# Pauses in the decode batches and the gates, sums of squares on a third engine, and another last norm in a one-layer hybrid decoder step

## The chip, the cores and the metric

The kernel runs on one core of a Trainium2 chip. The core has a matmul engine (PE, with its weight loads shown apart as PEld), a vector engine (DVE), a scalar engine (ACT), GpSimd (POOL), a queue engine (SP) and 16 DMA engines. The metric is the device time of one execution in microseconds (us), the median of several runs.

## The reference

One inference step of one decoder layer: a half-weight SwiGLU FFN, a combined projection into mLSTM heads (4 of 128) and sliding-window attention (8 heads of 64, window 128), an output projection, and a second half-weight FFN, each with an RMSNorm before and after it. 1024 prompt rows and 8 decode sequences of 4 rows go through the same weights; D_MODEL is 1024, D_FF 2816. All is float32.

```python
def half_ffn(x, j, gpre, gpost):
    y = swiglu(rmsnorm(x, g[gpre]), ffn_w_gate[l, j], ffn_w_up[l, j], ffn_w_down[l, j])
    return x + 0.5 * rmsnorm(y, g[gpost])

x = half_ffn(x, 0, 0, 1)
h = rmsnorm(x, g[2])
(qm, km, vm, om, ip, fp), (qa, ka, va) = split_proj(h, w_in[l], b_gate[l])
u_m, new_m = mlstm_heads(qm, km, vm, om, ip, fp, mstate, mlstm_norm_gain[l], h.dtype)
u_a, new_kv = swa_prompt(...)            # swa_sample(...) for the decode rows
u = jnp.concatenate([u_m, u_a], axis=-1)
x = x + rmsnorm(u @ w_out[l], g[3])
x = half_ffn(x, 1, 4, 5)
```

The mLSTM of the decode rows starts from a given state C (128x128) and n for each of 8 sequences and 4 heads, reads it (q @ C) and writes the new one:

```python
num = a[..., None] * jnp.einsum('bhtk,bhkv->bhtv', q, C) + jnp.einsum('bhts,bhsv->bhtv', S, v)
C_new = decay[..., None, None] * C + jnp.einsum('bhs,bhsk,bhsv->bhkv', wk, k, v)
```

## The kernel before

The 1056 rows stand in columns, in four quarters q0 to q3 of 264 (256 of the prompt and 8 of decode), with the 1024 features over partitions in pairs of blocks (kp 0 to 3, tiles of 128x528). A float32 product is made of three passes of a faster float format, from a high and a low part of each operand (xh, xl for rows, wh, wl for weights), so most matmuls come in threes, all through one helper line, L163. Transposes have L160, the split into parts L206 (ACT, the high part) and L207 (DVE, the low part).

The phases are FFN1 (tiles gu, pd, and pl where a product waits for late rows), the middle or mix (pz, pv and po are columns of the input projection, for z, v and the output gate; sws, swp and swo are the attention; E, S, intra, inter and U the mLSTM of the prompt; pw is the output projection, of uh and ul, the parts of the head outputs), FFN2, and the last norm.

What stands where on an engine is set by a hand-made clock (class `Order`). Each side job is a generator that is given a start and yields a number of us of PE time. Every matmul that the main loop issues moves the clock on by its price, and side jobs that are due are stepped in between, so a `yield 2.6` means that some 2.6 us of matmuls of the main loop come before the job goes on. The engines then run their instructions in order, and wait for each other by semaphores. `issue_after` is an order alone: an instruction isn't placed ahead of another on its engine.

The jobs that the change touches:

- `post()` ends a phase for a quarter q: residual add (y, L606 and L607), squares on ACT, their sum over kp in `acc` (sq, L615), the halves (L250), the sums over partitions on PE with the rows turned (cs) and a reduce on DVE (L260), a reciprocal square root by two Newton steps in `rstd()` (L280 to L289, tiny operations; "newton" below), and its broadcast over partitions on PE (rb). The next phase's quarter waits for that row. `late` is true for all quarters of phase 2 (end of the mix) and for q2 and q3 of phase 1 (end of FFN1).
- `gates()` makes the decays of the mLSTM for a group of four chunks; each chunk has two transposes (gT) and a copy into `K.cols`.
- `mlstm_sample()` runs the decode rows of the mLSTM over pairs of sequences: read (sinter, from the states Cb), then for each pair of heads the update (sU on PE, L1885 on DVE). After the four pairs comes a head (sintra, snum, a norm, shT), and its turned result is copied by ACT (L1915) into the columns of z that later become uh and ul.
- `Last.finish()` is the tail after the last matmul of FFN2.

```python
            for b, ps, Cb in zip(bs, pu, C):
                for x in range(2):
                    h = 2 * hp + x
                    nc.vector.scalar_tensor_tensor(Cb[:, h], Cb[:, h], K.dec[:, 1, h, b:b + 1],
                                                   ps[:, x * 129:(x + 1) * 129], op0=ALU.mult, op1=ALU.add)
            yield BW
```

Of the kernel before, what the change touches and what calls it, by code (L numbers as in the profile page):

```python
# [14 lines left out]
ALU = mybir.AluOpType  # L15
# [27 lines left out]

BW = 2.4

# [13 lines left out]
def setup(ctx, tc, A, O):  # L59
# [17 lines left out]

    K.h, K.room = {}, 1000
    K.ident = K.cp.tile([P, P], F32, tag="ident", name="ident")
    make_identity(nc, K.ident)  # L80
# [99 lines left out]
def pair(t):  # L180
    return t.rearrange("p (a t) -> p a t", a=2)
# [18 lines left out]
def small(K, name, w):  # L200
    return K.kp.tile([P, 8], F32, tag="c", name=nm(K, name), bufs=16)[:, 0:w]
# [71 lines left out]

def rstd(K, ss, scale=1.0 / D, eps=EPS, root=False):


    nc = K.nc
    w = ss.shape[-1]
    v, r, t, u = [small(K, x, w) for x in ("v", "r", "rt", "ru")]
    nc.vector.tensor_scalar(v, ss, scale, eps, op0=ALU.mult, op1=ALU.add)  # L280
    nc.vector.tensor_scalar(r.bitcast(I32), v.bitcast(I32), -0.5, float(0x5F3759DF), op0=ALU.mult, op1=ALU.add)

    nc.vector.tensor_tensor(t, r, v, op=ALU.mult)
    nc.vector.tensor_tensor(t, t, r, op=ALU.mult)
    nc.vector.scalar_tensor_tensor(u, t, -10.0 / 3.0, t, op0=ALU.add, op1=ALU.mult)
    nc.vector.scalar_tensor_tensor(r, u, 5.0, r, op0=ALU.add, op1=ALU.mult)
    nc.vector.scalar_tensor_tensor(t, r, -0.5 * 0.375 ** 3, v, op0=ALU.mult, op1=ALU.mult)
    nc.vector.tensor_tensor(t, t, r, op=ALU.mult)
    nc.vector.scalar_tensor_tensor(r, t, 1.5 * 0.375, r, op0=ALU.add, op1=ALU.mult)  # L289
    if not root:  # L290
        return r
    nc.vector.tensor_tensor(u, v, r, op=ALU.mult)
    return r, u
# [288 lines left out]
def post(K, phase, q, y, acc, half, nxt, gpre=None):  # L582
# [22 lines left out]
    for kp in range(4):  # L605
        nc.vector.tensor_tensor(pair(y[kp]), pair(y[kp]), cr.unsqueeze(1).to_broadcast([P, 2, QW]), op=ALU.mult)  # L606
        nc.vector.tensor_tensor(y[kp], y[kp], x[kp], op=ALU.add)  # L607
        if nxt:
            stash(K, q, kp, y[kp])
            sq = tmp(K, "sq", 2 * QW)  # L610
            nc.scalar.square(sq, y[kp])
            if acc is None:
                acc = sq
            else:
                nc.vector.tensor_tensor(acc, acc, sq, op=ALU.add)  # L615
        if nxt == "mix":
# [15 lines left out]
    yield PW[3]  # L632
    r = rstd(K, col_stats(K, sq, phase))
    yield PW[4][late]
    if nxt == "mix":
# [36 lines left out]
class Last:  # L672
# [30 lines left out]
    def block(self, mo, ps):  # L703
# [14 lines left out]
        if mo == 6:  # L718
            K.od.spawn(self.stats(0), 2.0)
        if mo == 3:  # L720
# [3 lines left out]

    def stats(self, i):

        ss = col_stats(self.K, self.acc[i], 3)
        if i:
            self.K.nc.vector.tensor_tensor(ss, ss, self.ss, op=ALU.add)
        self.ss = ss  # L730
        yield 0
# [21 lines left out]

    def finish(self):
        K, q = self.K, self.q
        for _ in self.stats(1):
            pass
        K.od.drain()

        c = rstd(K, self.ss, 4.0 / D, 4.0 * EPS)  # L760
        for j in range(3):
            for x in range(2):
                o = tmp(K, "yo", 512)
                if j < 2:
                    K.nc.vector.scalar_tensor_tensor(o, self.y[j][x], c[:, j:j + 1], self.x[j][x], op0=ALU.mult,
                                                     op1=ALU.add)
                    dst = K.O["y_prompt"][0, (2 * q + j) * P:(2 * q + j + 1) * P]
                else:
                    r = slice(96, P)
                    K.nc.scalar.activation(o[r], self.y[j][x][r], AF.Copy, scale=c[r, j:j + 1])  # L770
                    K.nc.vector.tensor_tensor(o[r], o[r], self.x[j][x][r], op=ALU.add)
                    o = o[120:128]
                    dst = K.O["y_sample"].rearrange("b t d -> (b t) d")[8 * q:8 * q + 8]
                K.nc.sync.dma_start(dst[:, x * 512:(x + 1) * 512], o)

# [618 lines left out]
def gates(K, n):  # L1394
# [28 lines left out]
    for c, o in chunks:  # L1423
        ps = bank(K, "gT", "b")
        pe(K, ps[:, 0:100], G[0:100, o:o + P], K.ident[0:100, 0:100], tr=True)
        pe(K, ps[:, P:P + 4], I[:, o:o + P], K.ident[0:4, 0:4], tr=True)
        nc.vector.tensor_copy(K.cols[:, c], ps[:, 0:160].rearrange("p (y s) -> p y s", s=32)[:, :, 0:4])
    K.od.done.add(("gates", n))

# [393 lines left out]
def mlstm_sample(K):  # L1823
# [41 lines left out]
    for b0 in range(0, 8, 2):  # L1865
# [3 lines left out]
        for b, Cb in zip(bs, C):  # L1869
            for h in range(HM):  # L1870
                q = qm[h // 2][:, (h % 2) * 256 + b * 32:(h % 2) * 256 + b * 32 + 32]
                pe(K, pi[32 * h:32 * h + 32, 0:129], q, Cb[:, h], start=(b == 0), stop=(b == 7),
                   tile_position=(0, 32 * h))
        for hp in range(2):
            pu = [bank(K, "sU", "ba"[hp]) for b in bs]
# [6 lines left out]
            for b, ps, Cb in zip(bs, pu, C):  # L1882
                for x in range(2):
                    h = 2 * hp + x
                    nc.vector.scalar_tensor_tensor(Cb[:, h], Cb[:, h], K.dec[:, 1, h, b:b + 1],  # L1885
                                                   ps[:, x * 129:(x + 1) * 129], op0=ALU.mult, op1=ALU.add)
            yield BW
        for b, Cb in zip(bs, C):
# [323 lines left out]
```

## Time and profile before

| | us |
|---|---|
| median of 3 runs | 1978.07 (1975.69 to 1980.95) |
| the profiled execution | 1979.65, its span 1977.9 |
| PE busy | 1953.1 (99% of the span) |
| DVE busy | 1251.7 (63%) |
| ACT busy | 903.9 (46%) |
| POOL busy | 42.9 (2%) |

The mean granted clock of PE is 0.993 of full speed. In the profile an engine's row says how long it was occupied; matmuls overlap, so the durations of single ones (0.28 us) are longer than the distance from one to the next. A view by windows gives busy time, the clock and the DMA share for each stretch of time. In the order of an engine below, a name's number tells tiles of the same kind apart, and x2 means two alike in a row.

### The profile page before, as it was taken

To read this page: it belongs to the slowest core of one execution; us is meant where nothing else is said; L and a number is where in the kernel's file an instruction comes from. 1 tells how busy PE (TensorE), PEld (TensorE's weight loads), DVE (VectorE), ACT (ScalarE), POOL (GpSimd) and SP (SyncE) were. 2 spreads that over 40 slices of the span, in tenths; PEclk is the share of its full clock that TensorE was granted. 3 is DMA by queue.
4 is the path that set the end of the run, shared out by engine and by line. 5 is a ranking of instruction groups with operands and counts; after the bars stand their busy time and mean duration, and the time that the engine had idled before them with its cause. 6 is when DMAs were issued, how large, how long until landed. Compare 5 with 4: busy or idle time off the path is not lost.

```text
span 1977.9 us, 40244 instructions
## 1 busy us (share of the span) xinstructions
PE 1953.1 (99%) x15897; PEld 1912.3 (97%) x15897; DVE 1251.7 (63%) x2986; ACT 903.9 (46%) x2167; POOL 42.9 (2%) x193
## 2 busy tenths in 40 slices
PE   8999999999999999999999999999999999999998
PEld 8999999999999999987999999999999999999997
DVE  8755555557568437467565768985555555856774
ACT  7533333336456332356244665353333334645563
POOL 1000000000000002000101000000000000000000
PEclk9999999999999999999999899999999999999999
DMA  7123222226357352201224234322222222746693
GB/s 251 55 76 116 92 76 84 74 92 207 97 161 240 109 146 84 63 1 38 79 65 131 64 108 136 121 84 91 76 89 86 97 76 82 218 122 199 206 265 121
DMA packets 283583, 226.42 MB, mean 114 GB/s; under 512 B 22441, under 2 KB 256033, under 8 KB 283393
## 3 DMA queue, kind: packets, MB, share of 16 engines
q1 hardware_dynamic: 283392, 223.84, 36.6%
q8 instruction: 124, 2.03, 0.4%
q14 instruction: 67, 0.54, 0.1%
HBM read 175.70 MB, written 47.89 MB: 113 GB/s over the span
## 4 chain that ended last, share of the span: by engine, by line
PE 91%; DVE 4%; ACT 2%; DMA 1%; issue 1%; SPq 0%; DVEq 0%; ACTq 0%
PE gu L163 41%; PE pd L163 25%; PE pz L163 6%; PE pw L163 4%; PE pl L163 3%; PE pv L163 3%; PE po L163 3%; DMA hq<-h 1%; PE sws L163 1%; PE swo L163 1%; PE yT L160 1%; ACT sws L1524 0%; PE swp L160 0%; PE U L163 0%; DVE y L607 0%
## 5 line engine op out<-in xcount | busy, mean ns | idle before, releaser
L163 PE MATMUL gu<-Xh,wh 128*128 128x264 f32 x2240 | 636.0, 284 | 1.5 <-ACT sc L1023 1.5
L163 PE MATMUL gu<-Xl,wh 128*128 128x264 f32 x2240 | 636.9, 284 | 0.0
L163 PE MATMUL gu<-Xh,wl 128*128 128x264 f32 x2240 | 636.2, 284 | 0.0
L163 PE MATMUL pd<-hq,wh 128*128 128x264 f32 x2752 | 509.3, 286 | 1.2 <-ACT sc L1127 1.2
L163 PEld LDWEIGHTS pd<-hq,wh 128*128 128x128 f32 x2752 | 426.7, 188 | 1.8 <-ACT sc L1127 1.6
L163 PEld LDWEIGHTS gu<-Xh,wh 128*128 128x128 f32 x2240 | 421.7, 188 | 2.0 <-ACT sc L1023 1.9
L163 PEld LDWEIGHTS gu<-Xh,wl 128*128 128x128 f32 x2240 | 421.7, 188 | 0.0
L163 PEld LDWEIGHTS gu<-Xl,wh 128*128 128x128 f32 x2240 | 421.0, 188 | 0.0
L207 DVE TENSOR_TENSOR wl<-raw,wh 128x512 fp32r<-128x512 f32 (+1 forms) x442 | 289.7, 667 | 163.1 <-ACT wh L206 144.4
L163 PE MATMUL pd<-hq,wl 128*128 128x264 f32 x1376 | 391.4, 284 | 0.0
L206 ACT CAST wh<-raw 128x512 fp32r<-128x512 f32 (+1 forms) x442 | 259.9, 601 | 248.8 <-PE pd L163 103.9
L163 PEld LDWEIGHTS pd<-hq,wl 128*128 128x128 f32 x1376 | 258.7, 188 | 0.0
L1023 ACT COPY sc<-gu 128x264 f32<-128x264 f32 x240 | 91.0, 380 | 354.1 <-PE gu L163 334.0
L207 DVE TENSOR_TENSOR wl<-ws,wh 128x512 fp32r<-128x512 f32 x192 | 130.5, 689 | 91.3 <-ACT wh L206 87.8
L1034 DVE TENSOR_TENSOR h<-gu,sc 128x264 f32<-128x264 f32 x120 | 51.8, 432 | 137.1 <-PE gu L163 86.0
L206 ACT CAST wh<-ws 128x512 fp32r<-128x512 f32 x192 | 115.0, 622 | 7.0 <-DVE ws L800 5.8
L1040 DVE TENSOR_TENSOR sc<-gu,sc 128x264 f32<-128x264 f32 x120 | 51.7, 431 | 95.9 <-PE gu L163 47.9
L163 PE MATMUL pz<-xh,wh 128*128 128x264 f32 x352 | 102.9, 292 | 0.6 <-DVE z L2085 0.6
L163 PE MATMUL pz<-xl,wh 128*128 128x264 f32 x352 | 101.3, 288 | 0.0
L163 PE MATMUL pz<-xh,wl 128*128 128x264 f32 x352 | 101.3, 288 | 0.0
L1035 ACT ACTIVATE h<-h 128x264 f32<-128x264 f32 x120 | 51.0, 425 | 107.7 <-DVE h L1034 107.7
L206 ACT CAST hq<-hq 128x264 fp32r<-128x264 f32 x192 | 70.9, 412 | 23.0 <-DMA hq<-h 19.4
(420 smaller groups left out, 3051.8 us busy)
## 6 DMA issues: line engine op xcount, KB each, us to landing
raw<-ffn_w_down SPq DMA_DIRECT2D x64, 512.0 KB
h<-h SPq DMA_DIRECT2D x84, 264.0 KB
raw<-ffn_w_gate SPq DMA_DIRECT2D x42, 512.0 KB
raw<-ffn_w_up SPq DMA_DIRECT2D x42, 512.0 KB
hq<-h SPq DMA_DIRECT2D x160, 132.0 KB
raw<-ffn_w_down SPq DMA_DIRECT2D x40, 384.0 KB
x<-xs SPq DMA_DIRECT2D x48, 264.0 KB
raw<-w_in SPq DMA_DIRECT2D x21, 512.0 KB
```

What stands on the lines that cost most here:

```text
L160: K.nc.tensor.transpose(out, lhsT, rhs)
L163: ins = K.nc.tensor.matmul(out, lhsT, rhs, start=start, stop=stop, **kw)
L206: K.nc.scalar.copy(hi, src)
L207: (eng or K.nc.vector).tensor_tensor(lo, src, hi.bitcast(F32), op=ALU.subtract)
L1023: nc.scalar.copy(sc[n][:, g], ps)
L1034: nc.vector.tensor_tensor(d, bk[tg, g], sc[n][:, g], op=ALU.add)
L1035: nc.scalar.activation(d, d, AF.Silu)
L1040: nc.vector.tensor_tensor(sc[n][:, g], src, sc[n][:, g], op=ALU.add)
```

## The change

Five edits. The decode batches pause also between read and update (2.6), and 1.9 instead of 2.4 after each half of the update. The gates pause 1.0 after each chunk. In `post()`, where rows are wanted soon (`late`), the adds of the squares of kp 1 and 2 go from DVE to POOL, and in q3 the multiply and the residual add of a kp stand behind the newton of q2, if that has been written by then. The last norm sums the squares over partitions by three matmuls against a column of ones and takes the earlier sum in as a ready-made column (`rest`), writes its first prompt chunk in two halves, and does the decode rows first, with POOL for the add and ACT's queue for the DMA.

```diff
...
 NP = [1.6, 3.0]
 GW = 10.0
-BW = 2.4
+BW = [2.6, 1.9]
 NPLAIN = 1
...
     K.X, K.b, K.S = [None] * NQ, [None] * NQ, [None] * NG
     K.h, K.room = {}, 1000
+    K.chain = None
     K.ident = K.cp.tile([P, P], F32, tag="ident", name="ident")
     make_identity(nc, K.ident)
     K.ones = K.cp.tile([P, 1], F32, tag="ones", name="ones")
...
     return ps[:, 0:QW]
-def rstd(K, ss, scale=1.0 / D, eps=EPS, root=False):
+def rstd(K, ss, scale=1.0 / D, eps=EPS, root=False, rest=None):
     nc = K.nc
     w = ss.shape[-1]
     v, r, t, u = [small(K, x, w) for x in ("v", "r", "rt", "ru")]
-    nc.vector.tensor_scalar(v, ss, scale, eps, op0=ALU.mult, op1=ALU.add)
+    if rest is None:
+        nc.vector.tensor_scalar(v, ss, scale, eps, op0=ALU.mult, op1=ALU.add)
+    else:
+        nc.vector.scalar_tensor_tensor(v, ss, scale, rest, op0=ALU.mult, op1=ALU.add)
     nc.vector.tensor_scalar(r.bitcast(I32), v.bitcast(I32), -0.5, float(0x5F3759DF), op0=ALU.mult, op1=ALU.add)
     nc.vector.tensor_tensor(t, r, v, op=ALU.mult)
...
     nc.vector.scalar_tensor_tensor(r, u, 5.0, r, op0=ALU.add, op1=ALU.mult)
     nc.vector.scalar_tensor_tensor(t, r, -0.5 * 0.375 ** 3, v, op0=ALU.mult, op1=ALU.mult)
     nc.vector.tensor_tensor(t, t, r, op=ALU.mult)
-    nc.vector.scalar_tensor_tensor(r, t, 1.5 * 0.375, r, op0=ALU.add, op1=ALU.mult)
+    K.newton = nc.vector.scalar_tensor_tensor(r, t, 1.5 * 0.375, r, op0=ALU.add, op1=ALU.mult).ins
     if not root:
         return r
     nc.vector.tensor_tensor(u, v, r, op=ALU.mult)
...
     acc = None
     g, i = q // 2, q % 2
     for kp in range(4):
-        nc.vector.tensor_tensor(pair(y[kp]), pair(y[kp]), cr.unsqueeze(1).to_broadcast([P, 2, QW]), op=ALU.mult)
-        nc.vector.tensor_tensor(y[kp], y[kp], x[kp], op=ALU.add)
+        with K.tc.issue_after(K.chain) if late and q == 3 and K.chain else nullcontext():
+            nc.vector.tensor_tensor(pair(y[kp]), pair(y[kp]), cr.unsqueeze(1).to_broadcast([P, 2, QW]), op=ALU.mult)
+            nc.vector.tensor_tensor(y[kp], y[kp], x[kp], op=ALU.add)
         if nxt:
             stash(K, q, kp, y[kp])
             sq = tmp(K, "sq", 2 * QW)
...
             if acc is None:
                 acc = sq
             else:
-                nc.vector.tensor_tensor(acc, acc, sq, op=ALU.add)
+                e = nc.gpsimd if kp < 3 and late else nc.vector
+                e.tensor_tensor(acc, acc, sq, op=ALU.add)
         if nxt == "mix":
             for k in (2 * kp, 2 * kp + 1):
                 s = slice((k % 2) * QW, (k % 2) * QW + QW)
...
     sq = halves(K, acc, phase)
     yield PW[3]
     r = rstd(K, col_stats(K, sq, phase))
+    K.chain = K.newton if late and q == 2 else None
     yield PW[4][late]
     if nxt == "mix":
         rc = K.kp.tile([P, 3], F32, tag=f"rc{q}", name=nm(K, "rc"), bufs=1)
...
             self.acc.append(sq)
         nc.scalar.activation(y, ps, AF.Copy, scale=gain)
         if mo == 6:
-            K.od.spawn(self.stats(0), 2.0)
+            K.od.spawn(self.stats(), 2.0)
         if mo == 3:
             K.od.spawn(self.first(self.t), 5.0)
         elif mo > 3:
             K.od.spawn(self.second(mo, y), 3.0)
-    def stats(self, i):
-        ss = col_stats(self.K, self.acc[i], 3)
-        if i:
-            self.K.nc.vector.tensor_tensor(ss, ss, self.ss, op=ALU.add)
-        self.ss = ss
+    def stats(self):
+        ss = col_stats(self.K, self.acc[0], 3)
+        self.rest = small(self.K, "ss", 3)
+        self.K.nc.vector.tensor_scalar(self.rest, ss, 4.0 / D, 4.0 * EPS, op0=ALU.mult, op1=ALU.add)
         yield 0
     def first(self, t):
...
         yield 0
     def finish(self):
         K, q = self.K, self.q
-        for _ in self.stats(1):
-            pass
+        nc = K.nc
+        ss = sbank(K, "cs")
+        for j, w in enumerate(WIN):
+            pe(K, ss[:, j:j + 1], self.acc[1][:, w:w + P], K.ones)
         K.od.drain()
-        c = rstd(K, self.ss, 4.0 / D, 4.0 * EPS)
-        for j in range(3):
+        c = rstd(K, ss[:, 0:3], 4.0 / D, rest=self.rest)
+        r = slice(96, P)
+        ys = K.O["y_sample"].rearrange("b t d -> (b t) d")[8 * q:8 * q + 8]
+        o = [tmp(K, "yo", 512) for _ in range(2)]
+        for x in range(2):
+            nc.scalar.activation(o[x][r], self.y[2][x][r], AF.Copy, scale=c[r, 2:3])
+        for x in range(2):
+            nc.gpsimd.tensor_tensor(o[x][r], o[x][r], self.x[2][x][r], op=ALU.add)
+            nc.scalar.dma_start(ys[:, x * 512:(x + 1) * 512], o[x][120:128])
+        for j in range(2):
+            dst = K.O["y_prompt"][0, (2 * q + j) * P:(2 * q + j + 1) * P]
             for x in range(2):
                 o = tmp(K, "yo", 512)
-                if j < 2:
-                    K.nc.vector.scalar_tensor_tensor(o, self.y[j][x], c[:, j:j + 1], self.x[j][x], op0=ALU.mult,
-                                                     op1=ALU.add)
-                    dst = K.O["y_prompt"][0, (2 * q + j) * P:(2 * q + j + 1) * P]
-                else:
-                    r = slice(96, P)
-                    K.nc.scalar.activation(o[r], self.y[j][x][r], AF.Copy, scale=c[r, j:j + 1])
-                    K.nc.vector.tensor_tensor(o[r], o[r], self.x[j][x][r], op=ALU.add)
-                    o = o[120:128]
-                    dst = K.O["y_sample"].rearrange("b t d -> (b t) d")[8 * q:8 * q + 8]
-                K.nc.sync.dma_start(dst[:, x * 512:(x + 1) * 512], o)
+                for a in ((0, 256), (256, 512)) if j + x == 0 else ((0, 512),):
+                    f = slice(*a)
+                    nc.vector.scalar_tensor_tensor(o[:, f], self.y[j][x][:, f], c[:, j:j + 1], self.x[j][x][:, f],
+                                                   op0=ALU.mult, op1=ALU.add)
+                    nc.sync.dma_start(dst[:, x * 512 + a[0]:x * 512 + a[1]], o[:, f])
...
         pe(K, ps[:, 0:100], G[0:100, o:o + P], K.ident[0:100, 0:100], tr=True)
         pe(K, ps[:, P:P + 4], I[:, o:o + P], K.ident[0:4, 0:4], tr=True)
         nc.vector.tensor_copy(K.cols[:, c], ps[:, 0:160].rearrange("p (y s) -> p y s", s=32)[:, :, 0:4])
+        yield 1.0
     K.od.done.add(("gates", n))
...
                 q = qm[h // 2][:, (h % 2) * 256 + b * 32:(h % 2) * 256 + b * 32 + 32]
                 pe(K, pi[32 * h:32 * h + 32, 0:129], q, Cb[:, h], start=(b == 0), stop=(b == 7),
                    tile_position=(0, 32 * h))
+        yield BW[0]
         for hp in range(2):
             pu = [bank(K, "sU", "ba"[hp]) for b in bs]
             for x in range(2):
...
                     h = 2 * hp + x
                     nc.vector.scalar_tensor_tensor(Cb[:, h], Cb[:, h], K.dec[:, 1, h, b:b + 1],
                                                    ps[:, x * 129:(x + 1) * 129], op0=ALU.mult, op1=ALU.add)
-            yield BW
+            yield BW[1]
         for b, Cb in zip(bs, C):
             nc.gpsimd.tensor_copy(nn[:, b], Cb[:, :, P])
             nc.sync.dma_start(O["s_C"][0, b].rearrange("h k v -> k h v"), Cb[:, :, 0:P])
```

PE in the middle of the decode batches, before. kw and vs make the update sU, Cb and qm the read sinter; po is the main loop's projection of the output gate.

```order
L163 MATMUL sinter_14003<-Cb_13917,qm_13995 32x129 x2
L163 MATMUL sinter_14003<-Cb_13917,qm_13999 32x129 x2
L163 MATMUL sU_14126<-vs,kw_13962 128x129 x2
L163 MATMUL sU_14127<-vs,kw_13962 128x129 x2
L163 MATMUL po_14104<-xh_1538_9805,wh_13753 128x264
L163 MATMUL sU_14136<-vs,kw_13962 128x129 x2
L163 MATMUL po_14104<-xl_1539_9806,wh_13753 128x264
L163 MATMUL po_14104<-xh_1538_9805,wl_13754 128x264
```

And the like place after:

```order
L164 MATMUL sU_14106<-vs,kw_13960 128x129
L164 MATMUL sU_14107<-vs,kw_13960 128x129
L164 MATMUL sU_14106<-vs,kw_13960 128x129
L164 MATMUL sU_14107<-vs,kw_13960 128x129
L164 MATMUL po_14072<-xh_1558_9876,wh_13757 128x264
L164 MATMUL po_14072<-xl_1559_9877,wh_13757 128x264
L164 MATMUL po_14072<-xh_1558_9876,wl_13758 128x264
L164 MATMUL po_14120<-xh_1530_9777,wh_13753 128x264
L164 MATMUL po_14120<-xl_1531_9778,wh_13753 128x264
L164 MATMUL po_14120<-xh_1530_9777,wl_13754 128x264
L164 MATMUL po_14120<-xh_1532_9781,wh_13753 128x264
L164 MATMUL po_14120<-xl_1533_9782,wh_13753 128x264
```

Before, sinter and sU follow each other with one or two po between them; after, a group of four sU is followed by a run of 12 po, of which the first eight are shown.

ACT behind shT, before, from the last copy out of it. num and hn belong to the prompt's mLSTM, og to the output gate, wh to a weight:

```order
L1915 COPY z_13851<-shT_14361 128x2x8
L206 CAST wh_14521<-raw_14517 128x512
L1760 ACTIVATE num_14407<-inter_14411,cols 128x129
L206 CAST uh_14403<-z_12798 128x528
L1760 ACTIVATE num_14407<-inter_14411,cols 128x129
L206 CAST wh_14525<-raw_14517 128x512
L206 CAST uh_14421<-z_12863 128x528
L206 CAST uh_14438<-z_12928 128x528
L1760 ACTIVATE num_14407<-inter_14431,cols 128x129 x2
L206 CAST uh_14454<-z_12993 128x528
```

After, from the last copy again:

```order
L1930 COPY z_13851<-shT_14449 128x2x8
L1774 ACTIVATE num_14495<-inter_14499,cols 128x129
L2076 ACT_TABLE_LOAD
L2076 ACTIVATE og_14287<-og_14287 128x528
L207 CAST uh_14491<-z_12780 128x528
L1774 ACTIVATE num_14495<-inter_14499,cols 128x129
L1696 ACTIVATE hn_14559,mss_14561<-num_14403 128x128
L207 CAST uh_14509<-z_12863 128x528
L1696 ACTIVATE hn_14559,mss_14561<-num_14403 128x128
L207 CAST wh_14715<-raw_14711 128x512
L207 CAST uh_14526<-z_12928 128x528
```

The casts uh that make the head outputs are now behind a table load and an og, and stand among the num and hn. On PE the shT stands as follows, after:

```order
L164 MATMUL pw_14598<-uh_13948,wh_14067 128x264
L164 MATMUL pw_14598<-ul_13949,wh_14067 128x264
L164 MATMUL pw_14598<-uh_13948,wl_14068 128x264
L164 MATMUL intra_14496<-v_10478,E_14347 128x129
L164 MATMUL intra_14496<-v_10482,E_14347 128x129
L164 MATMUL pw_14598<-uh_13967,wh_14067 128x264
L161 MATMUL shT_14449<-ident,snum_14376 128x128
L164 MATMUL pw_14598<-ul_13968,wh_14067 128x264
L164 MATMUL inter_14499<-C,z_13647 128x129
L164 MATMUL pw_14598<-uh_13967,wl_14068 128x264
L164 MATMUL pw_14598<-uh_13980,wh_14067 128x264
```

Before, some 90 rows of PE stood between shT and the first pw; now shT stands behind the first four pw, and pw of the decode heads' uh_14491 comes 25 rows after it.

DVE at the start of FFN2 (the sums of q2's squares, and the reduce and first step of q1's newton), before:

```order
L615 TENSOR_TENSOR sq_16323<-sq_16323,sq_16354 128x528
L992 TENSOR_TENSOR h_16149<-h_16149,pl_16253 128x264
L615 TENSOR_TENSOR sq_16323<-sq_16323,sq_16372 128x528
L260 TENSOR_REDUCE ss_16329<-cs_16325 128x3
L615 TENSOR_TENSOR sq_16323<-sq_16323,sq_16388 128x528
L280 TENSOR_SCALAR v_16331<-ss_16329 128x3
L992 TENSOR_TENSOR h_16195<-h_16195,pl_16300 128x264
L250 TENSOR_TENSOR sq_16323<-sq_16323 128x264
```

And after:

```order
L1005 TENSOR_TENSOR h_16149<-h_16149,pl_16253 128x264
L261 TENSOR_REDUCE ss_16329<-cs_16325 128x3
L622 TENSOR_TENSOR sq_16323<-sq_16323,sq_16388 128x528
L282 TENSOR_SCALAR v_16331<-ss_16329 128x3
L1005 TENSOR_TENSOR h_16195<-h_16195,pl_16300 128x264
L251 TENSOR_TENSOR sq_16323<-sq_16323 128x264
L285 TENSOR_SCALAR r_16332<-v_16331 128x3
L287 TENSOR_TENSOR rt_16333<-r_16332,v_16331 128x3
```

The two adds of kp 1 and 2 are gone from DVE (they are on POOL), and the third add, of kp 3, stands between q1's reduce and the first step of its newton.

## The prediction

> **What bounds the kernel now.** I read the busy times first, then the chain that ended last, then the waits of PE, and last the windows in which the granted clock falls.
>
> ```profile
> PE 1953.1 (99%) x15897; PEld 1912.3 (97%) x15897; DVE 1251.7 (63%) x2986; ACT 903.9 (46%) x2167; POOL 42.9 (2%) x193
> PE 91%; DVE 4%; ACT 2%; DMA 1%; issue 1%; SPq 0%; DVEq 0%; ACTq 0%
> ```
>
> PE is busy for 1953.1 of the 1977.9 us of the span and carries 91% of the chain. The change takes no matmul of weight off PE, so it can win in three places only: where PE waits, where PE runs at half clock, and in the tail after the last matmul. The waits of PE, all of the span:
>
> ```profile
> PE rb L160 <- DVE r L289: 3.2, 5, 1.5
> PE cs L160 <- DVE sq L250: 2.0, 1, 2.0
> PE pz L163 <- DVE z L2085: 0.6, 1, 0.6
> PE sU L163 <- DVE Cb L1885: 0.5, 1, 0.5
> ```
>
> The columns are total, times and longest. These are the waits on which the change acts, 6.3 us together: the stats of a norm (cs, rb), a projection (pz) and the decode states (sU). The half clock costs as much. Busy times by window; PEclk is the third number from the end:
>
> ```profile
> core 0: us, PE busy (x) PEld busy (x) DVE busy (x) ACT busy (x) POOL busy (x), PEclk, DMA share, GB/s
> 956.57:959.98 3.41, 3.41 (x23) 2.74 (x22) 0.89 (x5) 0.28 (x2) 0.00 (x0) 1.00 0.64 181
> 959.98:963.39 3.41, 3.41 (x18) 3.29 (x17) 2.37 (x20) 0.00 (x0) 0.19 (x1) 0.50 0.20 52
> 1086.27:1089.68 3.41, 3.41 (x35) 2.58 (x35) 2.39 (x10) 0.00 (x0) 0.38 (x2) 1.00 0.75 221
> 1089.68:1099.92 10.24, 10.24 (x63) 9.12 (x64) 3.43 (x12) 0.59 (x1) 0.76 (x4) 0.50 0.32 97
> 1260.36:1263.77 3.41, 0.84 (x7) 0.66 (x7) 3.39 (x9) 1.65 (x3) 0.00 (x0) 1.00 0.63 238
> 1263.77:1267.18 3.41, 3.41 (x18) 3.41 (x17) 3.41 (x8) 0.63 (x1) 0.00 (x0) 0.50 0.00 0
> ```
>
> Three stretches run at 0.50: 3.41 us at the gates, 10.24 us in the decode batches, 3.41 us at the start of FFN2. Half the time in each is lost: 1.7, 5.1 and 1.7 us. Before the third, PE was nearly idle (0.84 of 3.41). Before the other two it reads as busy, so I looked at what was in them, the full-width po matmuls alone:
>
> ```profile
> 1082.86:1086.27 3.41, 1.51 (x8) 1.10 (x8) 0.00 (x0) 1.00 0.82 239
> 1086.27:1089.68 3.41, 0.90 (x3) 0.48 (x3) 0.00 (x0) 1.00 0.75 221
> ```
>
> With 8 po matmuls in a window the next one kept the full clock; with 3 (and 32 narrow ones of the decode states) it lost it. My reading is that narrow matmuls count for little in whatever grants the clock. It rests on these two windows.
>
> **The change, part by part.** All against the profiled execution: 1979.65 us, span 1977.9; this is 1.6 above the median of the runs, 1978.07.
>
> *Decode batches.* The pauses put 9 to 12 po matmuls between the groups of sinter and sU, where there were 1 to 3. A full-width matmul comes every 0.12 us (1128.34 to 1128.46 below), so by the order every 3.41 us would hold about 12, more than the 8 that kept the clock. Taken: the 10.24 us stretch goes, −5.1 (ends: 0 if it stays, −5.1). The sU wait goes too, −0.5 (row above).
>
> *What the longer batches push back.* The decode head (shT) now stands inside the first pw matmuls. Before, it had 15 us of po matmuls behind it:
>
> ```profile
> 1113.50 0.33 PE L160 MATMUL shT<-ident,snum 128*128 128x128 f32 x1
> 1128.34 0.28 PE L163 MATMUL pw<-uh,wh 128*128 128x264 f32 x1
> 1128.46 0.28 PE L163 MATMUL pw<-ul,wh 128*128 128x264 f32 x1
> 1106.01 1.28 ACT L2061 ACT_TABLE_LOAD   x1
> 1107.31 0.64 ACT L2061 ACTIVATE og<-og 128x528 f32<-128x528 f32 x1
> 1113.92 0.71 ACT L1915 COPY z<-shT 128x16 f32<-128x16 f32 x8 [0.17 <-PE shT L160]
> 1116.70 0.62 ACT L206 CAST uh<-z 128x528 fp32r<-128x528 f32 x1
> 1117.38 0.37 ACT L1760 ACTIVATE num<-inter,cols 128x129 f32<-128x129 f32 x1
> 1121.61 0.31 ACT L1682 ACTIVATE hn<-num 128x128 f32<-128x128 f32 x1
> 1122.51 0.70 DVE L207 TENSOR_TENSOR ul<-z,uh 128x528 fp32r<-128x528 f32 x1
> ```
>
> Now ACT has, from shT: 0.42 to the first copy, copies 0.71, num 0.37, a table load 1.28 with og 0.64 (a like pair stood ahead of shT before, at 1106.01), and uh 0.62: first uh at +4.0. PE has 20 pw matmuls (2.4 us) and eight small ones (E counts four; some 0.1 each) until it needs it: 3.2. It stalls 0.8. For the other three heads ACT has three more casts, three hn (0.31, some 0.43 with the read of its sum), two num and one weight cast of 0.62: some 4.5, then the last ul 0.70: +9.2. PE's 32 rows to there hold 20 pw and 12 small ones, 3.9; it arrives at 7.1. Stall in all about 2.1. I take +2.0 (ends: 0, if ACT overlaps more; +8.0, if PE gets only the 3.2 done ahead of a chain of 11.2, the 9.3 us from 1113.92 to the last ul at 1123.21 with the table load and og put in). shT itself stands 7 rows behind a U that DVE takes first (C, then snum): another +0.3. What hid all this before was the po work, which is spent in the batches.
>
> *Gates.* A pause of 1.0 puts pz matmuls between the gT transposes of the chunks. The pz matmuls of the window before the 959.98 drop:
>
> ```profile
> 956.57:959.98 3.41, 1.02 (x4) 0.61 (x4) 0.00 (x0) 1.00 0.64 181
> ```
>
> Four, as poor as the po window above; it should now hold more, −1.7 (ends: 0, −1.7). The gates of the decode rows go some 90 rows back in the order of PE; the batches that read them start 600 rows later, so that costs nothing, and without that cover a transpose and its copy, under 1 us.
>
> *Rows wanted soon, phase 1.* The last y of q3 goes behind the newton of q2 on DVE, and two adds per quarter go to POOL.
>
> ```profile
> 768.25 0.70 DVE L606 TENSOR_TENSOR y<-y,cr 128x528 f32<-128x528 f32 x1
> 769.41 0.39 PE L163 MATMUL pz<-xh,wh 128*128 128x264 f32 x1 [0.55 <-DVE z L2085]
> 772.88 0.15 DVE L289 SCALAR_TENSOR_TENSOR r<-rt,r 128x3 f32<-128x3 f32 x1
> ```
>
> That newton ended at 772.88 because a y, an add and a square stood between its 0.15 us steps, each 0.70. Without them it ends some 3 us earlier, and the pz stall of 0.55 (its z stood behind the y of 768.25) goes: −0.6 (ends: 0, −1.2 with the two other rb waits around). The delayed y leaves the next stats where they were: 0.
>
> *Rows wanted soon, phase 2 (start of FFN2).* The same adds on POOL, but no reordering: in phase 2 the y loop of q3 is written before the newton of q2 exists.
>
> ```profile
> L207 POOL TENSOR_TENSOR wl<-w,wh 128x512 fp32r<-128x512 f32 x2 | 2.6, 1292 | 12.1 <-ACT wh L206 8.7 <-DMA xt<-x_prompt 3.4
> 1247.20 0.70 DVE L615 TENSOR_TENSOR sq<-sq,sq 128x528 f32<-128x528 f32 x1
> 1252.29 0.51 PE L160 MATMUL rb<-ident,r 128*128 128x128 f32 x3
> 1260.88 0.51 PE L160 MATMUL rb<-ident,r 128*128 128x128 f32 x3 [1.07 <-DVE r L289]
> 1263.44 0.58 PE L160 MATMUL cs<-ident,sq 128*128 128x128 f32 x3 [2.04 <-DVE sq L250]
> ```
>
> An add costs 0.70 on DVE and about 1.33 on POOL (1.292 x 528/512, the one two-input row POOL has). DVE gives up two adds per quarter, 1.4, but its third add now waits for two POOL adds in a row, 2.7 from 1246.8, when their squares are there; the newton of q1 stands behind it. That newton ends 0.3 later than before, for the rb of 1252.29, while PE reaches this rb ten pl matmuls (1.2 us) sooner: a wait of about 1.7 where there was next to none. The newton of q2 gains the 1.4 back, so that its rb (1260.88) hardly waits, and the cs of q3 (1263.44) still waits about 2.0. PE is the bound, so what counts is the sum of the waits: 3.5 to 3.9 before, 3.9 after. Taken: 0 (ends: −1, +2.5). For the half clock behind it: the idle time now falls in pieces with pl matmuls between, so it may not come; half of 1.7, −0.8 (ends 0, −1.7).
>
> The Trainium skill prices this move (GPSIMD Engine Reference, sections 3.1 and 4.1): a two-input elementwise add on GpSimd takes about twice as long as on VectorE, and such adds belong on VectorE. The ratio here, 1.33 to 0.70, agrees. By that rule alone the edit is a loss of 1.3 us on DVE's queue per quarter; by the rows it takes 1.4 off DVE and adds 1.3 to a chain that is late anyway, which is my 0.
>
> *Last norm.* The tail after the last pd:
>
> ```profile
> 1968.72 0.56 DVE L260 TENSOR_REDUCE ss<-cs 128x3 f32<-128x384 f32 x1 [6.67 <-PE cs L160]
> 1969.32 0.16 DVE L729 TENSOR_TENSOR ss<-ss,ss 128x3 f32<-128x3 f32 x1
> 1969.51 0.17 DVE L280 TENSOR_SCALAR v<-ss 128x3 f32<-128x3 f32 x1
> 1971.29 2.74 DVE L765 SCALAR_TENSOR_TENSOR yo<-yT,r,xT 128x512 f32<-128x512 f32 x4
> 1971.35 1.42 ACT L770 ACTIVATE yo<-yT,r 32x512 f32<-32x512 f32 x2 [2.89 <-DVE r L289]
> 1974.06 1.29 DVE L771 TENSOR_TENSOR yo<-yo,xT 32x512 f32<-32x512 f32 x2
> ```
>
> The reduce (0.60 to the next) and the add (0.19) go, since three matmuls against ones give the sums: r comes 0.8 earlier, at 1970.5. The four yo then end at 1973.25 instead of 1974.03, and their DMAs follow. The sample rows: ACT 0.71, then two POOL adds of at most 1.3 each, to 1973.8, where DVE ended at 1975.35; two DMAs by ACT's queue. The end moves by the prompt's 0.8 plus a little for the half chunk sent first: −1.0 (ends: 0 if the DMAs are the limit, −1.6 if the sample rows were).
>
> **Sum:** −5.1 −0.5 +2.0 +0.3 −1.7 −0.6 −0.8 −1.0 = −7.4. 1979.65 − 7.4 = 1972.2 us.
>
> **Rivals.** Each is measured against that sum.
> (a) The clock drop in the decode batches stays. For it: PE already reads 3.41 of 3.41 busy before it, so spreading may not be what matters. Against it: the 8 and 3 po matmuls above. It gives back 5.1: 1977.3. The Trainium skill says (TensorE: Matmul & The Clock Gate, Part 1 and the last section) that the clock halves after an idle window of about 3.4 us and that one should leave no idle gap over 3 us. The trace shows no idle time at 1086 at all, so the rule as written gives no reason for the drop or for its going.
> (b) The pw stall does not come: ACT's num and hn find gaps, and the waits of FFN2 fall apart enough for the full clock there: 2.3 and 0.9 less, 1969.0. For it: DVE and ACT have idle time here. Against it: the table load stands right on the chain.
> (c) Slower than before: the pw stall takes its upper end, +8.0 instead of 2.3 (+5.7), and PE, as idle as in 1260.36 to 1263.77, loses the clock for two or three windows after it (1.7 each, 3.4 to 5.1). 1981.3 to 1983.0. It makes the whole change slower than the median from an excess of 5.9 on. For it: every head needs ACT twice and DVE twice in a fixed order. Against it: 40 pw matmuls are mixed into the chain.
> (d) The POOL adds hold the newton of q1 longer than worked out, at their end of +2.5: 1974.7; if DVE's own instructions slow down beside POOL too, 1976.
>
> **How the numbers follow.** A measurement of this kernel tells a change of about 0.3%, 5.9 us, from none: faster is below 1972.1, slower above 1984.0. Chances: the sum 0.45, (a) 0.22, (b) 0.16, (c) 0.07, (d) 0.10. The sum's own range is 1969 to 1976, and 1972.2 sits on the bound, so half of it is faster; with all of (b) and a little of (d) faster has 0.42. Slower has 0.05, the end of (c); the rest is the same, 0.53. The range leaves out 2 in 10: low end 1967 (b with its ends), high end 1979, which takes in (a) and (d) and leaves (c).
>
> **What would show it.** Right: the granted clock is 1.00 from 1080 to 1103; no window at 0.50 near 960; PE waits of pw on ul and uh, 2 us together; no pz wait near 769; the first rb at the start of FFN2 waits 1.7, the last cs 2.0; no reduce in the tail and the first yo 0.8 after the end of the old one. Wrong: a stretch at 0.50 in the decode batches, or a pw wait above 4 us with half clock behind it, or the first FFN2 pl later than its place in the work before by over 1 us.

## The result: slower by 0.4%

| | median, us | lowest to highest | runs |
|---|---|---|---|
| before | 1978.89 | 1975.69 to 1984.30 | 11 |
| after | 1987.04 | 1984.10 to 1991.57 | 11 |

The ratio is 1.0038, with a 95% interval of 1.0029 to 1.0048: some 7.5 us slower, and above the predicted range. The profiled execution of the changed kernel has a span of 1989.8 us; the one before had 1977.9. Its time, 1991.57, is the longest of the eleven, so of the 11.9 us between the two traces some 4 belong to that execution alone (below).

PE's line of the page, after:

```profile
PE 1954.0 (98%) x15900; PEld 1912.9 (96%) x15900; DVE 1253.3 (63%) x2972; ACT 900.7 (45%) x2164; POOL 63.1 (3%) x207
```

PE does as much work as before (1953.1) in a longer span. POOL gained 20 us for 14 more instructions, twelve of them the adds of squares. The waits of PE, after (total, times, longest):

```profile
PE rb L161 <- DVE r L293: 8.5, 7, 2.4
PE pz L164 <- DVE z L2100: 3.4, 2, 1.9
PE gu L164 <- ACT sc L1036: 2.9, 2, 1.8
PE kcT L161 <- DMA kc<-cache_swa_k: 2.8, 2, 2.0
PE rb L161 <- DVE ss L261: 2.0, 1, 2.0
```

rb was 3.2 before and pz 0.6; kcT, the turned keys of the decode cache, did not wait at all. The last line, the rb behind ss, stands at 622 us, ahead of everything that the change moves. The wait of sU (0.5) is gone. The windows (PEclk is the third number from the end) show where the clock was halved, after:

```profile
core 0: us, PE busy (x) PEld busy (x) DVE busy (x) ACT busy (x) POOL busy (x), PEclk, DMA share, GB/s
971.86:978.69 6.83, 6.83 (x43) 6.09 (x42) 2.64 (x13) 1.14 (x4) 0.81 (x2) 0.50 0.46 125
1080.00:1105.00 25.00, 25.00 (x253) 22.33 (x251) 15.95 (x41) 10.66 (x18) 5.85 (x21) 1.00 0.71 198
1210.79:1214.21 3.42, 3.42 (x18) 3.42 (x17) 3.42 (x6) 2.18 (x5) 0.00 (x0) 0.50 0.70 228
1272.23:1279.06 6.83, 5.97 (x28) 6.00 (x29) 6.82 (x17) 1.90 (x3) 0.00 (x0) 0.50 0.11 42
```

The decode batches run at full clock, as forecast. But the stretch at the gates has doubled (6.83 for 3.41), and so has the one at the start of FFN2, and there is a new one at 1210.79, behind a rb that waited 2.4.

By matching the matmuls of the two traces, the changed kernel loses 2.2 us between 753 and 759 (phase 1), 1.1 between 790 and 896 (its cause is open), 3 to 4 between 957 and 991 (gates and decode attention), gains 7 through the decode batches up to the middle of pw, loses 3.7 at 1207 (rows of q0 and q1 after the mix), and 3.5 at the start of FFN2; the tail gains 0.4. A further loss, 3.7 at 622, is no work of the change: up to 750 us the order on every engine is the same as before, and there ACT waited for a weight of FFN1 to land. A last one, 2.0 to 2.5 near 1696, has a stretch of 3.41 us at half clock behind it that no other profiled execution here has; its cause is open.

What held DVE is seen beside the POOL adds. DVE and POOL in the changed kernel's timeline, at the rb of 1210 (start, duration, instruction; L290 and L291 are newton steps on 128x3):

```profile
1204.45 0.15 DVE L289 SCALAR_TENSOR_TENSOR ru<-rt 128x3 f32<-128x3 f32 x1
1204.60 3.61 POOL L622 TENSOR_TENSOR sq<-sq,sq 128x528 f32<-128x528 f32 x2 [91.53 <-ACT sq L617]
1205.14 1.30 DVE L290 SCALAR_TENSOR_TENSOR r<-ru,r 128x3 f32<-128x3 f32 x1
1206.97 1.27 DVE L291 SCALAR_TENSOR_TENSOR rt<-r,v 128x3 f32<-128x3 f32 x1
```

and in phase 1 (L631 takes 0.49 elsewhere):

```profile
754.37 1.33 POOL L622 TENSOR_TENSOR sq<-sq,sq 128x528 f32<-128x528 f32 x1 [4.86 <-ACT sq L617]
754.74 1.26 DVE L631 SCALAR_TENSOR_TENSOR xl<-y,gain,xh 128x264 fp32r<-128x264 f32 x1
757.56 1.38 POOL L622 TENSOR_TENSOR sq<-sq,sq 128x528 f32<-128x528 f32 x1 [1.86 <-ACT sq L617]
757.70 1.53 DVE L631 SCALAR_TENSOR_TENSOR xl<-y,gain,xh 128x264 fp32r<-128x264 f32 x1
```

A DVE instruction that reads SBUF twice and starts while POOL adds lasts until POOL is done and a little beyond: the newton steps end 0.02 us after the add, the L631 above 0.29 after it. So a newton step of 0.15 becomes 1.3. It works the other way too: the POOL add at 1204.60 took 1.82, against 1.33 for the one at 754.37, and the y of DVE that was running when it began ended at 1205.23, 0.63 into it. Instructions of DVE that read PSUM beside a POOL add kept their length (L1005, 0.42 at 1267.54).

### The profile page after: what moved, and what is told of

Read it like the earlier page. It is cut to its first block, busy times and chain, and to the rows that moved or that the text cites. A ratio compares the mean times of both kernels' runs of the same rounds, so it can differ in the third digit from the quotient of the medians.

```text
span 1989.8 us, 40274 instructions
## 1 busy us (share of the span) xinstructions
PE 1954.0 (98%) x15900; PEld 1912.9 (96%) x15900; DVE 1253.3 (63%) x2972; ACT 900.7 (45%) x2164; POOL 63.1 (3%) x207
## 3 DMA queue, kind: packets, MB, share of 16 engines
q8 instruction: 124, 2.03, 0.4%
## 4 chain that ended last, share of the span: by engine, by line
PE 89%; DVE 5%; DMA 3%; ACT 2%; issue 1%; POOL 0%; SPq 0%; POOLq 0%; DVEq 0%; ACTq 0%
PE gu L164 41%; PE pd L164 24%; PE pz L164 5%; PE pw L164 4%; PE pv L164 3%; PE pl L164 3%; PE po L164 2%; DMA hq<-h 1%; PE sws L164 1%; PE swo L164 1%; PE swp L161 1%; PE yT L161 1%; DVE y L613 0%; DMA raw<-ffn_w_down 0%; DMA kc<-cache_swa_k 0%
## 5 line engine op out<-in xcount | busy, mean ns | idle before, releaser
L207 ACT CAST wh<-raw 128x512 fp32r<-128x512 f32 (+1 forms) x442 | 260.0, 601 | 252.3 <-PE pd L164 107.0
L207 ACT CAST wh<-ws 128x512 fp32r<-128x512 f32 x192 | 115.0, 622 | 8.3 <-DVE ws L813 6.9
L207 ACT CAST hq<-hq 128x264 fp32r<-128x264 f32 x192 | 71.2, 412 | 24.1 <-DMA hq<-h 20.3
```

Source lines behind the costliest of these rows:

```text
L207: K.nc.scalar.copy(hi, src)
```

## The experiments

Each run was timed in five rounds beside the kernel before; ratios are to it. First the theory that the POOL adds are the loss (P), and its rival, that the pauses are (S).

**The adds back on DVE**, in the changed kernel:

```diff
-                e = nc.gpsimd if kp < 3 and late else nc.vector
-                e.tensor_tensor(acc, acc, sq, op=ALU.add)
+                nc.vector.tensor_tensor(acc, acc, sq, op=ALU.add)
```

> The changed kernel with the eight squares per late quarter pair added on DVE again (12 adds back from POOL); all else as changed. Theory P (the POOL adds are the loss: they hold DVE instructions that start beside them and lengthen the chain of the sums): the three places of the post jobs lose their +2.2, +3.7 and +3.5 us, so about 9.4 less than the changed kernel, 1977 to 1978, no more than the kernel before. Rival S (the pauses shift the order into a worse one, POOL costs at most 1.5): 1985 to 1986.

1976.58, ratio 0.9987 (0.9979 to 0.9996): against the 1.0038 of the changed kernel, some 10 us. P holds. The rb waits are back at 3.3 in all and pz no longer waits; kcT still waits 2.5.

**The adds on POOL alone**, in the kernel before (the same edit the other way):

> The kernel before with only the 12 adds moved to POOL. Theory P: +9 us, 1987 to 1989, with DVE instructions beside a POOL add drawn out from 0.15 or 0.49 to 1.1 to 1.6 us. Rival S: 0 to +1.5, 1979 to 1980.5.

1990.62, ratio 1.0063 (1.0047 to 1.0078): 12 us slower, above the 1987 to 1989 of theory P and far above the rival's 1980.5; the whole loss and more, from 12 adds whose time on POOL is 1.3 to 1.8 us each. The waits of PE in it:

```profile
PE rb L160 <- DVE r L289: 7.5, 7, 2.5
PE pz L163 <- DVE z L2086: 3.3, 2, 1.9
```

**The pauses of the decode batches alone**, in the kernel before (`BW = [2.6, 1.9]`, one more `yield`):

> The kernel before with only the pauses of the decode batches (2.6 and 1.9). If the decode batches gain what the changed trace shows there (10.7 us late before them, 3.5 after the pw start): -7, 1972. If the pauses are a loss later (pw start, S): 1978 to 1981. The granted clock should be 1.00 through the batches in both.

1974.47, ratio 0.9977 (0.9967 to 0.9986): −4.6 us, less than the −7 expected. The clock in it:

```profile
1080.00:1105.00 25.00, 25.00 (x257) 21.88 (x256) 16.83 (x48) 8.48 (x14) 1.98 (x8) 1.00 0.50 138
```

**POOL work beside DVE, with nobody waiting for it.** DVE keeps its adds; POOL adds each square onto itself after DVE has used it.

```diff
                 nc.vector.tensor_tensor(acc, acc, sq, op=ALU.add)
+                if kp < 3 and late:
+                    nc.gpsimd.tensor_tensor(sq, sq, sq, op=ALU.add)
```

> The kernel before with its DVE adds kept, and 12 extra POOL adds of the same shape, each of a square onto itself after DVE has used it; nobody reads what they make (they spoil nothing but a dead buffer). If POOL costs by holding DVE instructions beside it: some 12 of them drawn out by about 1 us each, +3 to +7 us, 1982 to 1986. If POOL costs only because the sums wait for two slow adds in a row: no change, 1979.

1991.91, ratio 1.0065 (1.0048 to 1.0082): 13 us, more than expected and as much as moving the adds. In the trace no instruction waits for what these adds make. So the longer chain of the sums, the only price that the prediction's sum and its range put on POOL, is not needed for the loss. DVE and POOL in it:

```profile
1204.93 1.46 POOL L617 TENSOR_TENSOR sq<-sq 128x528 f32<-128x528 f32 x1 [101.78 <-PE pw L163]
1205.38 1.02 DVE L287 SCALAR_TENSOR_TENSOR rt<-r,v 128x3 f32<-128x3 f32 x1
```

What of a POOL instruction holds DVE? The same with `nc.gpsimd.memset(sq, 0.0)`, and with `nc.gpsimd.tensor_copy(sq, sq)`:

> As the run with 12 extra POOL adds, but each a POOL memset of the same dead square (128x528, writes only, 0.54 us in the profile before). If what holds DVE is a POOL instruction that reads SBUF: DVE's two-input instructions keep their 0.15 to 0.7 us and the time is that of the kernel before, 1979. If any POOL instruction holds it: some 0.4 us for each of 12, +1 to +3, 1980 to 1982.

> As the run with 12 extra POOL memsets, but each a POOL copy of the same dead square onto itself (128x528, one SBUF input, written back), a little longer than a memset. If what holds DVE is that the POOL instruction reads SBUF: DVE's two-input instructions beside it are drawn out by up to its length of about 0.5 to 0.6 us and the time rises by 1 to 4 us. If it takes two inputs: 1979, as with the memsets.

The memsets cost nothing (1979.21, ratio 1.0000, 0.9991 to 1.0008), the copies 4.8 us (1983.68, ratio 1.0024, 1.0011 to 1.0036). The same newton step beside a memset, with another that lies wholly inside one (L284), and beside a copy:

```profile
1199.58 0.54 POOL L617 MEMSET sq<- 128x528 f32 x1 [103.67 <-PE pw L163]
1200.06 0.16 DVE L287 SCALAR_TENSOR_TENSOR rt<-r,v 128x3 f32<-128x3 f32 x1
754.00 0.54 POOL L617 MEMSET sq<- 128x528 f32 x1
754.33 0.15 DVE L284 TENSOR_TENSOR rt<-rt,r 128x3 f32<-128x3 f32 x1
```

```profile
1202.49 1.04 POOL L617 COPY sq<-sq 128x528 f32<-128x528 f32 x1 [101.79 <-PE pw L163]
1202.96 0.58 DVE L287 SCALAR_TENSOR_TENSOR rt<-r,v 128x3 f32<-128x3 f32 x1
```

So what holds a DVE instruction with two SBUF inputs is a POOL instruction that reads SBUF, with one input or two. Of the two that read, the longer costs more, 13 us for twelve adds and 4.8 for twelve copies; the memset, nearly as long as the shortest copy (0.54 and 0.62), costs nothing. This is what the Trainium skill states (SBUF — State Buffer, sections "SBUF: two separate sides" and "Who interferes with whom"): GpSimd's SBUF port pair is one that VectorE also uses for a second SBUF input, it is locked for a whole instruction, and the loser waits; two-input VectorE instructions are held only by a GpSimd instruction that reads SBUF. For two-input instructions these runs agree: the step L287 took 1.02 beside an add, 0.58 beside a copy and 0.16 beside a memset. The first newton step (L280, one input in SBUF) was held by all three: from 0.17 to 1.03 beside an add, to 0.59 beside a copy, and to 0.39 beside a memset:

```profile
751.51 0.54 POOL L617 MEMSET sq<- 128x528 f32 x1 [6.48 <-DVE sq L615]
751.69 0.39 DVE L280 TENSOR_SCALAR v<-ss 128x3 f32<-128x3 f32 x1
```

It ended 0.02 us after that memset. So this one instruction is held by a POOL instruction that only writes, too; it is the only one so held beside the twelve memsets, and the time does not show it.

**The pauses of the gates alone**, in the kernel before (`yield 1.0` after each chunk):

> The kernel before with only the pause of 1.0 after each gate chunk. Theory G (the pause moves the PE rows that read the decode caches, kcT, closer behind their DMAs and the slack is gone): PE waits of kcT on the DMA of about 2.5 to 3 us in all and a longer stretch at half clock there, +3, 1981.5. Rival (the prediction's term: the pz between the transposes keep the clock): -1.7, 1977.

1983.29, ratio 1.0020 (1.0010 to 1.0029): +4.0. Theory G is right in its sign and about in its size. The queue of SP and PE around the second half of the decode cache, before:

```profile
957.07 0.25 PE L160 MATMUL gT<-ident,G 100*128 100x100 f32 x1
957.15 0.41 SPq L1618 DMA_DIRECT2D kc<-cache_swa_k  x1
958.91 0.28 PE L160 MATMUL gT<-ident,G 100*128 100x100 f32 x1
962.61 0.98 PE L160 MATMUL kcT<-ident,kc 128*128 128x128 f32 x4
```

and with the pauses:

```profile
958.25 0.40 SPq L1619 DMA_DIRECT2D kc<-cache_swa_k  x1
962.42 0.95 PE L160 MATMUL kcT<-ident,kc 128*128 128x128 f32 x4 [2.29 <-DMA kc<-cache_swa_k]
964.88 0.37 PE L160 MATMUL gT<-ident,G 100*128 100x100 f32 x1
```

The four gT pairs had stood between the load and kcT. With the pauses they stand behind kcT, PE arrives 1.9 us after the issue instead of 5.5, and waits 2.29 for the load. The clock then halves:

```profile
959.17:962.58 3.41, 1.11 (x10) 0.94 (x10) 0.76 (x9) 0.62 (x1) 0.00 (x0) 1.00 0.61 179
962.58:972.82 10.24, 10.24 (x56) 8.55 (x55) 3.50 (x15) 1.76 (x6) 0.81 (x2) 0.50 0.36 100
```

**The pause in the first group of gates only** (`if n == 0`):

> The kernel before with the pause of 1.0 in the first group of gates only, not in the second, whose transposes stand between the second kc DMA and its kcT. If the +3.9 of the gate pauses is lost there: no kcT wait, 1979. If it is lost by pausing in general: 1981 to 1983.

1986.02, ratio 1.0032 (1.0021 to 1.0043). The expectation was wrong: the second group's transposes moved behind kcT here as well, and kcT waited 2.45. So the run does not part G from its rival; that a pause in one job moves the others was not allowed for.

**The cover given back**: the pauses kept, and a `yield 3.0` between the loads of the decode cache and kcT, in the kernel before and in the changed one without the POOL adds.

```diff
+        yield 3.0
         ps = bank(K, "kcT", "b")
```

> The kernel before with the pauses of 1.0 in the gates, and a pause of 3.0 between the DMA of the decode cache kc and its transposes kcT, so that other matmuls stand between them again. Theory G (the pause loses only because the gT transposes had stood between the kc DMA and kcT and hidden the load): no kcT wait on the DMA, no more half clock at 960 to 975 than before, 1979 or a little less. If the pauses lose by themselves: 1983 as with the pauses alone.

> The changed kernel with the adds back on DVE and the pause of 3.0 between the kc DMA and kcT. If POOL and the kcT wait are all that was lost: 1973 to 1974, as batches, newton order and last norm alone; with the half clock at 960 gone, 1972. If the gates lose otherwise: 1976.6 as without the pause.

In the kernel before: 1982.29, ratio 1.0012 (1.0000 to 1.0025), its runs spread from 1976.9 to 1984.6. The wait of the second kcT is gone, and its profiled execution has 3.41 us at half clock there; but that execution (1976.92) is the fastest of the twelve, and the median is only 1 us better than with the pauses alone, within the intervals: open. In the changed kernel without the adds: 1971.20, ratio 0.9956 (0.9938 to 0.9973), 6 us better than without the cover, and the fastest of all kernels here. kcT in it:

```profile
959.10 0.41 SPq L1631 DMA_DIRECT2D kc<-cache_swa_k  x1
962.91 0.69 PE L161 MATMUL kcT<-ident,kc 128*128 128x128 f32 x4
```

and its clock there:

```profile
959.64:963.05 3.41, 3.41 (x17) 3.14 (x17) 1.73 (x18) 0.62 (x1) 0.00 (x0) 0.50 0.62 184
```

This kcT does not wait. One stretch of 3.41 us at half clock is left there, as in the profiled execution of the kernel before, so neither trace with the pauses and the cover shows them doing what they were forecast to do. That stretch is no fixed cost either: three profiled executions of kernels without these pauses (the memsets, and the two further down with the decode adds on DVE and with half the pause in the batches) have none there.

**The other parts**: the last norm alone, the y of q3 behind the newton of q2 alone, and batches, newton and norm together.

> The kernel before with only the other last norm. The prediction's term: -1.0, 1977.5. From the changed trace the tail is 0.45 shorter, since the POOL adds of the decode rows hold the DVE products of the prompt: -0.5, 1978.

> The kernel before with only the y steps of q3 placed behind the newton of q2. The prediction's term: -0.6, with the pz wait of 0.7 near 769 gone, 1978. If the delayed y makes the next sums late instead: +0.3 to +0.6, 1979.

> The changed kernel without the POOL adds of squares and without the pauses of the gates, so batches, order behind the newton and last norm are left. If the gates cost about 3 and the others add up: 1973.5 to 1974. If the gates are no loss, the same as without the POOL adds alone: 1976.5.

1978.70 (ratio 0.9994, 0.9985 to 1.0003), 1978.52 (0.9992, 0.9983 to 1.0001) and 1973.79 (0.9972, 0.9962 to 0.9982). The first two can't be told from no change by their times. In the trace of the second the pz wait of 0.6 at 769 is gone and no wait takes its place. The three together give −5.5.

**The tail's decode adds on DVE**, after the prompt's products, in the kernel with those three parts:

> Batches, order behind the newton and the last norm, as in the run with those three, but the two adds of the decode rows on DVE behind the prompt's products instead of on POOL. If POOL holds a product of the prompt in the tail (1.2 instead of 0.75): the products end 0.46 earlier and the two adds (0.65 each, the DMAs behind them) take it back: 1973 to 1974, no product above 0.76. If the tail's length was POOL's own: 1.3 less, 1972.5.

1974.41, ratio 0.9972 (0.9964 to 0.9981): no difference. In its trace no product lasts above 0.75, as expected. In the changed kernel the products and POOL's adds stand against each other:

```profile
1983.10 3.33 DVE L785 SCALAR_TENSOR_TENSOR yo<-yT,r,xT 128x256 f32<-128x256 f32 x5
1983.94 2.95 POOL L777 TENSOR_TENSOR yo<-yo,xT 32x512 f32<-32x512 f32 x2 [714.95 <-ACT yo L775]
```

The five products take 3.33 for the four of 2.74 before, though they cover the same columns; one of them lasts 1.21.

**Half the pause in the batches** (1.3 and 1.9):

> The kernel before with pauses of 1.3 and 1.9 in the decode batches (5.1 us per pair, 4.8 before, 6.4 changed). If the density of full-width matmuls sets the clock: a stretch at half clock of 0 to 7 us stays, 1976 to 1978. If the split of the pause alone does it: as with 2.6 and 1.9, no half clock, 1974.5.

1976.94, ratio 0.9988 (0.9980 to 0.9997): −2.4, about half the gain. Its profiled execution has no half clock in the batches, so the one trace does not show the stretch that was expected; the time is in the expected range.

## Why the prediction was wrong

1. **The step that failed is the price of POOL** ("Rows wanted soon", phase 1 and phase 2). It counted 1.33 us per add on POOL and 0.70 saved on DVE, and the wait of the third add for the chain: 0 in the sum, +2.5 at the end of its range. The runs show that POOL's reading holds DVE's own instructions, and price the adds, with the half clock that follows the waits, at 10 us (taken out of the changed kernel) to 12 us (put into the kernel before). At the start of FFN2 the prediction had PE's waits at 3.9 and half the cost of the slow stretch gone; the trace has 5.6 (rb 2.03 and 1.92, cs 1.68) and a stretch twice as long. In phase 1 it had the pz wait gone; the trace has two, 1.4 and 1.9. The wait for two adds in a row that it did price is there too: DVE waits 1.8 for POOL at 1257. A row that shows the hold stood in the trace of before, beside the very POOL row that gave the 1.33:

```profile
28.05 1.29 POOL L207 TENSOR_TENSOR wl<-w,wh 128x512 fp32r<-128x512 f32 x1 [8.73 <-ACT wh L206]
27.71 1.92 DVE L537 SCALAR_TENSOR_TENSOR xb<-xr,gain,rrow 128x264 f32<-128x264 f32 x2
```

Two of these take 0.89 elsewhere. Rival (d) named the hold in half a sentence; its 1976 leaves 3.8 us for all that POOL costs, some 6 to 8 too little. The rule that the prediction weighed, on how long an add takes on each engine, is the lesser one here; and the 1.3 us per quarter that it called a loss on DVE's queue would be one of the chain of the sums, since the adds leave that queue.

   Two readings of the rows before were off as well. PE's waits at the start of FFN2 were 3.2 (0.12, 1.07 and 2.04), not 3.5 to 3.9. And of the 6.3 us of waits on which the change was said to act, 1.5 are an rb at 9.45, in the first norm, which the change does not touch.

2. **A place was left out.** The adds also run for q0 and q1 after the mix, at 1204 to 1210. For this place the sum has no term; the trace shows +3.7, of which 1.7 is the half clock after the longer rb wait.

3. **The gates had the wrong sign**: −1.7 forecast, +4.0 measured. The pause did move the transposes, but in the kernel before they had stood between the load of the decode cache and kcT. "That costs nothing" was worked out for those who read the transposes and not for the load that they covered. In all four profiled kernels with pauses there and no cover, kcT waits 2.5 to 3.0 in all, and 6.83 to 10.24 us at half clock lie there; in the trace with the pauses alone the stretch follows a window in which PE was busy for 1.11 of 3.41 us. Giving the cover back took 6 us off one kernel and about 1 off the other, so how much of the +4.0 this wait explains stays open. In the changed kernel without the adds the pauses cost about 3 (0.9987 with them, 0.9972 without); with pauses and cover it stands at 0.9956, but the intervals overlap, so a gain from covered pauses is not shown.

4. **The decode batches went the way that was forecast, and came near its size by luck.** −5.6 + 2.3 was forecast, −4.6 measured. The half clock goes, but neither number held. The stretch of 10.24 us was one draw: the ten profiled executions with the old batches had 13.65 us at half clock there twice, 10.24 three times, 3.41 four times and none once, 7.2 in the mean, so 3.6 lost; the six with the full pauses had none. And the stall at the start of pw did not come:

```profile
1130.47 0.62 ACT L207 CAST uh<-z 128x528 fp32r<-128x528 f32 x1
1131.16 0.37 PE L164 MATMUL pw<-uh,wh 128*128 128x264 f32 x1
```

ACT's chain took 3.8 us from shT, near the 4.0 worked out, but PE needed 3.9 to get there and not 3.2: its small matmuls between took longer than the 0.1 each assumed for them, so PE came just in time. (For the second stretch the prediction's own prices, 20 of 0.12 and 12 of 0.1, give 3.6 and not 3.9.) Rival (b) was right that the stall does not come, though not for its reason, gaps on ACT.

5. **The tail**: −1.0 forecast, 0.4 in the trace, and no difference that the times can show (−1.2, its interval holds 0). POOL's adds of the decode rows hold one of the prompt's products, the mechanism of point 1 again; moving them to DVE changed no time, so its price there is not shown.

6. **The newton order in phase 1**: −0.6 forecast, the pz wait it named is gone when the edit stands alone, and the time (−1.6, interval to +0.2) does not disagree.

The parts alone give 12.5 (adds) + 4.0 (gates) − 4.6 (batches) − 1.2 (norm) − 1.6 (newton) = +9.1, with intervals of about 2 us each; +7.5 was measured for all together.

Rival (a), that the half clock in the batches stays, is refuted: none of the six profiled executions with the full pauses showed any there. Rival (c) had the direction, slower at 1981.3 to 1983.0, but by a stall of pw, and no pw waits in the trace. In the chances, "a little of (d)" can't add to faster, since both its times lie above the bound of 1972.1; half of the sum and all of (b) make 0.39, not 0.42. Whether narrow matmuls count less in what grants the clock remains a reading: with 1.3 us pauses the clock held as well in the one trace.

## What to carry to other kernels

Before work goes to POOL because POOL is idle, look at what DVE does at that moment: in these runs an SBUF-reading instruction on POOL held DVE's two-input SBUF instructions for as long as it ran, and a chain of tiny steps such as a Newton iteration suffered most (0.15 us to 1.3). Before small work is spread out, ask what it covers where it stands: the transposes of the gates stood between a load and its reader, and without them the reader waited 2.3 us. And a stretch at half clock in one trace is a draw; look at a second execution before its whole loss is put into a sum.

## What was not expected of the hardware

Twelve POOL instructions of 128x528 that nobody waits for cost 13 us as adds, 4.8 us as copies and nothing as memsets. The hold is exact: the newton step that began 0.47 us into a copy ended 0.01 us after the copy (1202.96 + 0.58 = 1203.54; the copy ended at 1203.53). The POOL instruction waits for DVE as well: the copy issued at 1202.49 lasted 1.04, and a two-input DVE instruction had run until 1203.04 (L207, from 1202.36 for 0.68), which leaves 0.5 for the copy itself. POOL can wait much longer than for one instruction: an add that began at 1215.02, in the run where DVE keeps its adds, lasted 6.1 us. DVE ran its two-input instructions without a pause and at their usual length (0.70) until 1220.20, and the add was done 0.92 later.
